# The latents' MLP of a two-layer hybrid trunk: eight block products per projection, or Strassen's seven

## The chip, the cores and the metric

The kernel runs on one NeuronCore of one Trainium2 chip. The metric is device time in microseconds (us) for one launch. Before the change it was 3617.11 us, the median of 3 runs (3616.78 to 3617.87).

## What is computed

The reference is a trunk of two layers over 1024 latent tokens and 256 context tokens with 1024 features. Each layer has a token mixer and then an MLP; what matters here is the MLP, its norms and its residual:

```python
def sq_relu_mlp(h, w1, w2):                      # w1: 1024 x 4096, w2: 4096 x 1024
    return jnp.square(jax.nn.relu(h @ w1)) @ w2

# per layer, after the token mixer gave y_lat (and y_ctx in layer 0)
h_lat = h_lat + gate_a * rms_norm(y_lat, norm_g[layer, 1])
m_lat = modulate(rms_norm(h_lat, norm_g[layer, 2]), shift_m, scale_m)
h_lat = h_lat + gate_m * rms_norm(sq_relu_mlp(m_lat, w_mlp1, w_mlp2), norm_g[layer, 3])
if need_ctx:  # layer 0 only: the same for the 256 context tokens, modulated by c_ctx
    ...
```

## The kernel before, in words

Data are feature-major: a tile holds 128 features on the partitions and tokens along the free axis. The tokens are cut into three chunks: 0 is the context (256 tokens), 1 and 2 are the latents (512 each). Every large product is done in three matmuls of fp32r operands: a number is split into a high part (a cast on ScalarE, ACT) and a low part (the difference, on VectorE, DVE), and high x high, high x low and low x high are added up in PSUM.

A weight tile is 128 x 512 (four blocks of 128 x 128). `split_w` (L176 to L184) loads it into one of three buffers `raw` (DMA issued on SyncE, SP), casts it to `wh` (L182, ACT) and takes the difference `wl` (L183, on DVE in the MLP). It has two buffers each of `wh` and `wl`. `proj` (L186 to L195) uses a weight tile for 12 matmuls per chunk.

A layer's second half goes: output projection (`po`), the norm between (`norm_mid`: post-norm with residual, then pre-norm), the MLP, the norm at its end (`norm_end`). The MLP goes over the tokens in passes: in layer 0 chunk 1, then chunks 2 and 0 together, so that one split weight tile serves 12 matmuls of 512 columns and 12 of 256; in layer 1 chunk 1, then chunk 2. In a pass `up` (tile `pu`) makes one block of 128 hidden features from two weight tiles, squares the ReLU and splits the result into `hh` and `hl`; `down` (tile `pd`) takes groups of four hidden blocks into the eight output blocks `y`, which are added up in SBUF (L1378). Hidden features never leave the chip.

The order on each engine is set by a scheduler from priorities and a timeline of its own; `aside` (L1278) gives the norms a lower priority than the matmuls that follow them. At the end of layer 1 the last `down` of chunk 2 is done in two halves of 256 tokens, each with its weights split anew, and then the last norm and the output's DMA follow.

Of the kernel before, what the change touches and what calls it, by code (L numbers as in the profile page):

```python
# [17 lines left out]
D = 1024  # L18
LT = 1024
LC = 256  # L20
# [77 lines left out]
def _prep(i):  # L98
# [23 lines left out]
    o["w2"] = f["w_mlp2"].reshape(DEPTH, 8, 4, 128, KB, 128).transpose(0, 1, 4, 3, 2, 5)  # L122
# [18 lines left out]
def kernel(ctx: ExitStack, tc: tile.TileContext, a: dict, out: bass.AP, dbg=None):  # L141
# [34 lines left out]
    def split_w(src, eng, b=128):  # L176
        n = src.shape[1]
        raw = wp.tile([128, 512], F32, tag="raw", name="raw")
        nc.sync.dma_start(out=raw[:, :n], in_=src)
        wh = wp.tile([128, 512], F32R, tag="wh", name="wh", bufs=2)  # L180
        wl = wp.tile([128, 512], F32R, tag="wl", name="wl", bufs=2)
        S.copy(out=wh[:, :n], in_=raw[:, :n])  # L182
        eng.tensor_tensor(out=wl[:, :n], in0=raw[:, :n], in1=wh[:, :n].bitcast(F32), op=SUB)  # L183
        return [w[:, :n].rearrange("p (a b) -> p a b", b=b) for w in (wh, wl)]  # L184

    def proj(src, pss, xs, eng):  # L186
        """pss[ci] = src^T x over the 8 blocks of 128 features, in three products of the operands' parts"""
        for g in range(2):
            wh, wl = split_w(src[:, 4 * g:4 * g + 4].rearrange("p a b -> p (a b)"), eng)
            for ci, ps in pss.items():  # L190
                n = CHUNKS[ci][1]
                for k in range(4):
                    for j, (w_, x_) in enumerate(((wh, xs[ci][0]), (wh, xs[ci][1]), (wl, xs[ci][0]))):
                        P.matmul(out=ps[:, :n], lhsT=w_[:, k], rhs=x_[:, 4 * g + k, :n],  # L194
# [13 lines left out]
    def ada(l, g, ap_, pp, sbp=None):  # L208
# [9 lines left out]
        sb = sbp.tile([128, 512], F32, tag="t2", name="asb", bufs=4) if sbp else ap_.tile([128, 512], F32, tag="asb", name="asb", bufs=1)  # L218
# [25 lines left out]
    def nrsqrt(ps, n, scale, tile_):  # L244
        """-1 / sqrt(scale * ps + EPS): the table's value and a Newton step"""
# [5 lines left out]
        V.scalar_tensor_tensor(out=y[:, :n], in0=h[:, :n], scalar=1.5, in1=y[:, :n], op0=SUB, op1=MULT)  # L251
        return y

    def rstd_of(src, n, tile_, pp):
        accs = []
        for half in range(2):
# [3 lines left out]
            for b in range(4 * half + 1, 4 * half + 4):  # L260
                sq = tile_("sq")
                S.activation(out=sq[:, :n], in_=src(b), func=AF.Square)  # L262
                eng.tensor_tensor(out=acc[:, :n], in0=acc[:, :n], in1=sq[:, :n], op=ADD)  # L263
            accs.append(acc)
# [3 lines left out]
        return nrsqrt(ps, n, 1.0 / D, tile_)  # L268

    def prenorm(l, w, y, c, hi, lo, tile_, pp):  # L270
        n = y.shape[2]
        s1, sh = mods[l][3][w], mods[l][0][:, 24 * w:24 * w + 8]
        r = rstd_of(lambda b: y[:, b], n, tile_, pp)
        for b in range(KB):
            q = tile_("q")
            V.scalar_tensor_tensor(out=q[:, :n], in0=y[:, b], scalar=s1[:, b, c:c + 1], in1=r[:, :n], op0=MULT, op1=MULT)
            if b % 4 == 3:
                S.activation(out=q[:, :n], in_=q[:, :n], func=AF.Identity, bias=sh[:, b, c:c + 1])
                S.copy(out=hi[:, b], in_=q[:, :n])
                G.tensor_tensor(out=lo[:, b], in0=q[:, :n], in1=hi[:, b].bitcast(F32), op=SUB)  # L280
                continue
            S.activation(out=hi[:, b], in_=q[:, :n], func=AF.Identity, bias=sh[:, b, c:c + 1])  # L282
            V.scalar_tensor_tensor(out=lo[:, b], in0=q[:, :n], scalar=sh[:, b, c:c + 1],  # L283
                                   in1=hi[:, b].bitcast(F32), op0=ADD, op1=SUB)

    def postnorm(l, w, y, c, hsrc, tile_, pp):
        """y = hsrc + gate * normalized y"""
        n = y.shape[2]
        res = not isinstance(hsrc, bass.AP) or hsrc.shape[0] == 128
        gg = mods[l][4][w]  # L290
        r = rstd_of(lambda b: y[:, b], n, tile_, pp)
        for b in range(KB):
            if res:
                ht = hsrc[:, b]
            else:
                ht = tile_("ht")
                nc.sync.dma_start(out=ht[:, :n], in_=hsrc[b])
            q = tile_("q")
            V.scalar_tensor_tensor(out=q[:, :n], in0=y[:, b], scalar=gg[:, b, c:c + 1], in1=r[:, :n], op0=MULT, op1=MULT)  # L299
            G.tensor_tensor(out=y[:, b], in0=q[:, :n], in1=ht[:, :n], op=ADD)  # L300
# [18 lines left out]
    def gates(l, ap_, pool, prm):  # L319
        """raw [128, NU, 36] = dt(2,6) | a(2,6) | b(2,6) per token -> dt, a=dt*A, g, beta."""  # L320
# [1116 lines left out]
```

## Time and profile before

| | |
|---|---|
| median of 3 runs | 3617.11 us |
| profiled execution, span from its first to its last instruction | 3611.6 us |
| between that span and the median | 5.5 us |
| TensorE (PE) matmuls busy | 3329.6 us (92%), 21790 matmuls |
| DVE / ACT / GpSimd (POOL) busy | 2162.3 / 1606.0 / 1042.2 us |
| DMA | 497.96 MB, mean 138 GB/s |

The output projection and MLP of layer 0 run from about 880 to 1940 us, those of layer 1 from about 2754 us to the end. In both, PE's slices are at 8 and 9 tenths, and DVE's and ACT's at 2 to 6. A matmul's "busy" in this profile lasts from its issue to its modelled end, so that successive matmuls overlap: how many run in a stretch says what one costs, not the mean length of one.

### The profile page before, as it was taken

What the parts mean: (1) busy time and instruction counts of PE and PEld (TensorE: products, weight loads), DVE (VectorE), ACT (ScalarE), POOL (GpSimd) and SP (SyncE); (2) the same over time, 40 slices, a digit from 0 to 9 for tenths busy, and PEclk for the clock granted to TensorE, in tenths of its full rate; (3) what the DMA queues carried; (4) which work ended last, traced back from release to release, by engine and by line L of the source; (5) the groups of instructions that cost most, each with busy time, mean ns of one, the idle gap of its engine ahead of it and who ended that gap; (6) DMA issues with size and microseconds to landing.
All of it is one profiled execution on the core that took longest, in us unless ns stands there. A gap on an engine that the chain in (4) does not pass through costs nothing. (4 is left out here: it accounts for less than half of the span.)

```text
span 3611.6 us, 57569 instructions
## 1 busy us (share of the span) xinstructions
PE 3329.6 (92%) x21790; PEld 2648.5 (73%) x21790; DVE 2162.3 (60%) x3645; ACT 1606.0 (44%) x3059; POOL 1042.2 (29%) x993
## 2 busy tenths in 40 slices
PE   4998898999989999999998888888999899999997
PEld 2766786766866888888886566776677678877886
DVE  6668961487585446544438557982575764454445
ACT  4665533566463334322225465532665553333333
POOL 3238324574251001100005337533672420010002
PEclk8999999899999999999998899998999999999998
DMA  5467447664245333322223555636754333334333
GB/s 200 140 192 203 138 116 225 224 206 152 94 137 181 98 98 102 107 65 62 65 63 112 173 168 161 172 112 197 238 183 150 129 110 96 97 115 142 97 96 102
DMA packets 359324, 497.96 MB, mean 138 GB/s; under 512 B 62998, under 2 KB 220550, under 8 KB 359046
## 3 DMA queue, kind: packets, MB, share of 16 engines
q1 hardware_dynamic: 356166, 480.12, 43.0%
q0 software_dynamic: 2880, 14.16, 1.3%
q8 instruction: 171, 2.80, 0.3%
q14 instruction: 107, 0.88, 0.1%
HBM read 387.09 MB, written 107.07 MB: 137 GB/s over the span
## 5 line engine op out<-in xcount | busy, mean ns | idle before, releaser
L182 ACT CAST wh<-raw 128x512 fp32r<-128x512 f32 (+1 forms) x712 | 440.1, 619 | 1019.6 <-PE pd L1372 475.6
L183 DVE TENSOR_TENSOR wl<-raw,wh 128x512 fp32r<-128x512 f32 x592 | 425.2, 720 | 407.1 <-ACT wh L182 389.7
L263 POOL TENSOR_TENSOR nacc<-nacc,nsq 128x256 f32<-128x256 f32 (+1 forms) x105 | 95.6, 912 | 1468.8 <-ACT nsq L262 1466.2
L1372 PE MATMUL pd<-hh,wh 128*128 128x512 f32 (+1 forms) x1312 | 481.6, 367 | 11.2 <-DVE y L1378 7.2
L1372 PE MATMUL pd<-hh,wl 128*128 128x512 f32 (+1 forms) x1312 | 480.5, 368 | 7.3 <-DVE wl L183 7.3
L194 PE MATMUL pu<-th,wl 128*128 128x512 f32 (+1 forms) x1280 | 475.0, 371 | 11.8 <-DVE wl L183 11.8
L194 PE MATMUL pu<-th,wh 128*128 128x512 f32 (+1 forms) x1280 | 477.4, 373 | 7.0 <-ACT th L282 7.0
L1372 PE MATMUL pd<-hl,wh 128*128 128x512 f32 (+1 forms) x1312 | 479.2, 365 | 0.2 <-DVE hl L1360 0.2
L194 PE MATMUL pu<-tl,wh 128*128 128x512 f32 (+1 forms) x1280 | 475.2, 371 | 3.2 <-DVE tl L283 3.2
L194 PE MATMUL ps<-th,wh 128*128 128x512 f32 (+1 forms) x1144 | 440.8, 387 | 19.7 <-ACT ub L371 7.8
L194 PE MATMUL ps<-th,wl 128*128 128x512 f32 (+1 forms) x1144 | 430.6, 379 | 6.5 <-POOL wl L183 6.5
L194 PE MATMUL ps<-tl,wh 128*128 128x512 f32 (+1 forms) x1144 | 433.1, 379 | 0.0
L1378 DVE TENSOR_TENSOR y<-pd,y 128x512 f32<-128x512 f32 (+1 forms) x288 | 179.3, 624 | 305.2 <-PE pd L1372 305.0
L386 DVE SCALAR_TENSOR_TENSOR sil<-ub,cw,sil 128x256 f32<-128x256 f32 (+1 forms) x236 | 273.0, 1179 | 51.7 <-ACT sil L384 45.7
L183 POOL TENSOR_TENSOR wl<-raw,wh 128x512 fp32r<-128x512 f32 (+1 forms) x120 | 181.0, 1510 | 404.1 <-ACT wh L182 384.4
L1372 PEld LDWEIGHTS pd<-hh,wh 128*128 128x128 f32 x1312 | 249.5, 190 | 56.4 <-ACT wh L182 9.4
L1372 PEld LDWEIGHTS pd<-hh,wl 128*128 128x128 f32 x1312 | 249.1, 190 | 54.5 <-DVE wl L183 13.5
L194 PEld LDWEIGHTS pu<-th,wl 128*128 128x128 f32 x1280 | 243.0, 190 | 57.3 <-DVE wl L183 16.2
L194 PEld LDWEIGHTS pu<-th,wh 128*128 128x128 f32 x1280 | 243.4, 190 | 51.8 <-ACT th L282 7.8
L194 PEld LDWEIGHTS ps<-th,wh 128*128 128x128 f32 x1144 | 225.8, 198 | 73.5 <-issue 13.0
L1372 PEld LDWEIGHTS pd<-hl,wh 128*128 128x128 f32 x1312 | 249.6, 190 | 38.9 <-DVE hl L1360 0.4
L194 PEld LDWEIGHTS pu<-tl,wh 128*128 128x128 f32 x1280 | 243.2, 190 | 44.7 <-DVE tl L283 4.0
(291 smaller groups left out, 5946.1 us busy)
## 6 DMA issues: line engine op xcount, KB each, us to landing
raw<-in_w_dram SPq DMA_DIRECT2D x528, 256.0 KB
aw<-in_wada_dram SPq DMA_DIRECT2D x96, 512.0 KB
raw<-in_winf_dram SPq DMA_DIRECT2D x116, 256.0 KB
stp<-rt SPq DMA_DIRECT2D x36, 768.0 KB
raw<-in_wout_dram SPq DMA_DIRECT2D x64, 256.0 KB
rt<-st SPq DMA_DIRECT2D x72, 192.0 KB
crow<-rc POOLq DMA_DIRECT2D x36, 384.0 KB, 4.8
sr<-rs SPq DMA_DIRECT2D x18, 576.0 KB
```

The lines of the kernel that those rows point to most:

```text
L182: S.copy(out=wh[:, :n], in_=raw[:, :n])
L183: eng.tensor_tensor(out=wl[:, :n], in0=raw[:, :n], in1=wh[:, :n].bitcast(F32), op=SUB)
L194: P.matmul(out=ps[:, :n], lhsT=w_[:, k], rhs=x_[:, 4 * g + k, :n], start=(g + k + j == 0), stop=(g == 1 and k == 3 and j == 2))
L263: eng.tensor_tensor(out=acc[:, :n], in0=acc[:, :n], in1=sq[:, :n], op=ADD)
L386: V.scalar_tensor_tensor(out=acc, in0=u[:, o + k:o + k + n], scalar=w[:, bi, k:k + 1], in1=acc, op0=MULT, op1=ADD)
L1372: P.matmul(out=ps[:, :n], lhsT=w_[:, k], rhs=x_[:, o:o + n], start=(i == 0), stop=(i == 11))
L1378: V.tensor_tensor(out=y, in0=ps[:, :n], in1=y, op=ADD)
```

## The change

The latents' MLP is done by Strassen's scheme (Winograd's form): weights and tokens are cut in halves along both axes of a product, so that 7 products of quarter size, on sums of quarters, stand for 8. Chunks 1 and 2 are the two token halves. Context tokens no longer share weight tiles with chunk 2 and get a pass of their own with the old scheme (`up0`, `down0`) after the latents'.

For the inner layer's 16 pairs of hidden blocks, `up(i)` makes four sums of weight tiles on DVE (S1, S2, `A11`-`A21`, `A12`-S2) and up to seven products, with token operands B11, B21, B22, T1 to T4 that stay in SBUF. From the four results, which it squares, it makes the seven operands that the outer layer needs, and stores them to DRAM (`th`, 256 KB each). Two of the seven products (`begin`) need chunk 1 alone; for the first 8 (layer 0) or 10 (layer 1) pairs they are done ahead (`ahead`), beside the norms of chunk 2, and what doesn't fit in PSUM goes through DRAM (`tp`). The outer layer goes through 4 groups of 7 steps: a step loads a hidden operand of 1 MB from DRAM and splits it (`hidden`), makes sums of weights in SBUF (`make`), and does four weight tiles' products for all 512 columns.

```diff
+    def two(raw, eng, b=128):
...
+        pool = wps[0]
+        wps.append(wps.pop(0))
+        wh = pool.tile([128, 512], F32R, tag="wh", name="wh", bufs=2)
+        wl = pool.tile([128, 512], F32R, tag="wl", name="wl", bufs=2)
+        S.copy(out=wh[:, :n], in_=raw)
+        eng.tensor_tensor(out=wl[:, :n], in0=raw, in1=wh[:, :n].bitcast(F32), op=SUB)
...
+            def product(ps, wts, ops, first=True):
+                wh, wl = wts
+                for j in range(4):
+                    xh, xl = ops[j]
+                    for i, (w_, x_) in enumerate(((wh, xh), (wh, xl), (wl, xh))):
+                        P.matmul(out=ps, lhsT=w_[:, j], rhs=x_, start=first and j + i == 0, stop=(j == 3 and i == 2), skip_group_check=True)
...
+            def begin(i, A11, A12):
+                b1, b2 = bank(), bank()
+                product(b1, two(A11, V), B11)
+                p1 = granule("p1")
+                S.copy(out=p1, in_=b1)
+                if HELD <= i < BEGUN:
+                    nc.sync.dma_start(out=tp[l][i], in_=p1)
+                h11 = granule("h11")
+                product(b2, two(A12, V), B21)
+                V.tensor_tensor(out=h11, in0=b2, in1=p1, op=ADD)
+                square(h11, h11)
+                put_h(i, 0, h11)
...
+            def up(i, beside=lambda: None):
...
+                product(b1, two(S2, V), T2, False)
...
+                S.copy(out=h12, in_=b1)
...
+                product(b3, two(S1, V), T1)
...
+                S.copy(out=h22, in_=b3)
...
+                V.tensor_tensor(out=A11, in0=A11, in1=A21, op=SUB)
+                product(b1, two(A11, V), T3, False)
...
+                V.tensor_tensor(out=h22, in0=b1, in1=h22, op=ADD)
+                square(h22, h22)
+                put_h(i, 2, h22)
+                V.tensor_tensor(out=A12, in0=A12, in1=S2, op=SUB)
+                product(b3, two(A12, V), B22, False)
...
+            STEPS = ((0, 0, (0, 0), 0, "S1"), (1, 1, (0, 0), 1, "S2"), ("S2", 4, (1, 0), 0, "S3"), (0, 5, (1, 1), 0, None),
+                     (3, 6, (0, 1), 0, "S4"), ("S1", 3, (1, 1), 2, None), (1, 2, (1, 0), 2, None))
...
+                for m in range(4):
+                    ps = banks[bk][m]
+                    wts = two(W[g, w_][:, m], V)
+                    product(ps, wts, [[t[:, j] for t in ops2[g, k][1:]] for j in range(4)], fresh)
+                    if g == 0 and bk == 0:
+                        S.copy(out=y[:, m], in_=ps)
+                    else:
+                        V.tensor_tensor(out=y[:, m], in0=ps, in1=y[:, m], op=ADD)
+                    if m == 0 and beside:
+                        make(beside, g)
+                    if m in (0, 1) and n_ + 1 < len(todo):
+                        hidden(todo[n_ + 1][0], todo[n_ + 1][2], 2 * m)
+                if last and g == 3 and k == 6:
+                    aside(lambda: run(end(1, 0, 512, lat(1), nte)))
...
+                def down0(g):
+                    for m in range(KB):
+                        wh, wl = split_w(a["w2"][l, g // 2, 2 * (m // 4) + g % 2][:, m % 4].rearrange("p a b -> p (a b)"), V)
+                        for j in range(4):
+                            hh, hl = hid[8 * (g // 2) + 2 * j + g % 2]
+                            for i, (w_, x_) in enumerate(((wh, hh), (wh, hl), (wl, hh))):
...
+                                P.matmul(out=acc[m], lhsT=w_[:, j], rhs=x_, start=(g + j + i == 0 and m % 2 == 0),
+                                         stop=(g == 7 and j == 3 and i == 2), skip_group_check=True)
+                        if m % 2:
+                            run(both, 1)
```

`two` splits a weight tile or a sum that is in SBUF, with buffers from two pools in turn, so that four pairs of `wh` and `wl` are in use. `up` begins with four loads and S1 and S2. `both` is a generator: the end norms of chunks 1 and 2 (512 columns at a time, not 256 as before), a piece of which is emitted after each `up0` and every second output block of `down0`. Of the end of layer 1 the last norm now covers 512 tokens, and no weights are split twice. `split_w` keeps its three `raw` buffers.

Three places show how the order changed. On PE, in layer 0's outer layer before, each split weight tile served 512 columns of chunk 2 and then 256 of the context (`pd`, `hh` and `hl` are the hidden parts):

```order
L1372 MATMUL pd<-hl,wh 128x512
L1372 MATMUL pd<-hh,wl 128x512
L1372 MATMUL pd<-hh,wh 128x256
L1372 MATMUL pd<-hl,wh 128x256
L1372 MATMUL pd<-hh,wl 128x256
L1372 MATMUL pd<-hh,wh 128x256
```

The context's own pass in the changed kernel (`pu` is any PSUM bank of the MLP, `x` the context's operand parts, `nps` the sum of a latent chunk's norm):

```order
L204 MATMUL pu<-x_15658,wh 128x256
L204 MATMUL pu<-x_15659,wh 128x256
L204 MATMUL pu<-x_15658,wl 128x256
L295 MATMUL nps<-nacc,cst 128x512
L204 MATMUL pu<-x_15658,wh 128x256
```

There a weight tile is followed by 12 matmuls of 256 columns and no others. On SP in layer 0's MLP before, the queue held weight loads almost alone (`hl` and `hm` are the residual stream in DRAM):

```order
L179 DMA raw<-in_w_dram 128x512
L1313 DMA hl_96<-y 128x8x256
L179 DMA raw<-in_w_dram 128x512 x3
L1293 DMA res<-hm_95 128x8x512
L179 DMA raw<-in_w_dram 128x512 x115
```

In the changed kernel's inner layer, in the same queue, for pairs 11 to 13 of layer 0 (`A` a weight load; `th` a store, of h11, h22, u1, u2, h12, h21, u4):

```order
L1421 DMA th_118<-u_12712 128x512
L1412 DMA A<-in_w_dram 128x512
L1421 DMA th_119<-h_12769 128x512
L1412 DMA A<-in_w_dram 128x512 x2
L1421 DMA th_121<-h_12829 128x512
L1412 DMA A<-in_w_dram 128x512
L1421 DMA th_122<-u_12872 128x512
L1421 DMA th_123<-u_12873 128x512
L1421 DMA th_124<-h_12810 128x512
L1421 DMA th_120<-h_12897 128x512
L1421 DMA th_125<-u_12874 128x512
L1412 DMA A<-in_w_dram 128x512
```

The four loads of a pair now stand between seven stores, each of which waits for a result. On DVE in the outer layer before (`wl` a weight tile's low part, `y` a sum from PSUM):

```order
L1378 TENSOR_TENSOR y<-pd,y 128x512
L1378 TENSOR_TENSOR y<-pd,y 128x256
L183 TENSOR_TENSOR wl<-raw,wh 128x512
L1378 TENSOR_TENSOR y<-pd,y 128x512
L1378 TENSOR_TENSOR y<-pd,y 128x256
```

One step of the outer layer in the changed kernel (`x` is the low part of the next hidden operand, `S_14646` a sum of weights, `xb` the outputs and the weights):

```order
L193 TENSOR_TENSOR wl<-xb,wh 128x512
L1581 TENSOR_TENSOR S_14646<-S_14563,xb 128x1024 x2
L1650 TENSOR_TENSOR xb<-pu,xb 128x512
L193 TENSOR_TENSOR wl<-xb,wh 128x512
L1650 TENSOR_TENSOR xb<-pu,xb 128x512
L193 TENSOR_TENSOR wl<-xb,wh 128x512
L1596 TENSOR_TENSOR x<-x 128x1024 x2
L1650 TENSOR_TENSOR xb<-pu,xb 128x512
L193 TENSOR_TENSOR wl<-xb,wh 128x512
L1650 TENSOR_TENSOR xb<-pu,xb 128x512
```

Besides a difference and a sum per weight tile there are now two to four operations of 1024 columns per step, for the sums of weights and the split of the next operand.

## Rows read from the trace of the kernel before

**Rows 1.** The page, by engine: busy us (share of the span) xinstructions
```profile
PE 3329.6 (92%) x21790; PEld 2648.5 (73%) x21790; DVE 2162.3 (60%) x3645; ACT 1606.0 (44%) x3059; POOL 1042.2 (29%) x993
```

**Rows 2.** Stretches of the MLP: us, busy (xinstructions) by engine, clock, DMA share, GB/s
```profile
1200.00:1300.00 100.00, 100.00 (x443) 82.81 (x442) 48.28 (x74) 33.08 (x55) 0.00 (x0) 1.00 0.32 98
1700.00:1800.00 100.00, 100.00 (x576) 88.23 (x575) 42.29 (x73) 23.88 (x44) 0.00 (x0) 1.00 0.20 63
```

**Rows 3.** PE's groups by form: shapes xcount | busy us, mean ns | idle before
```profile
L194 PE MATMUL pu<-th,wh 128*128 128x512 f32 x1024 | 404.9, 395 | 7.0 <-ACT th L282 7.0
...
L1372 PE MATMUL pd<-hh,wh 128*128 128x512 f32 x992 | 388.5, 392 | 3.0 <-ACT wh L182 2.8
...
L1372 PE MATMUL pd<-hh,wh 128*128 128x256 f32 x320 | 93.1, 291 | 8.1 <-DVE y L1378 7.2 <-ACT wh L182 0.8
...
L194 PE MATMUL pu<-th,wh 128*128 128x256 f32 x256 | 72.5, 283 | 0.0
```

**Rows 4.** DVE's groups by form, whole span
```profile
L183 DVE TENSOR_TENSOR wl<-raw,wh 128x512 fp32r<-128x512 f32 x592 | 425.2, 720 | 407.1 <-ACT wh L182 389.7 <-DMA raw<-in_wout_dram 5.1 <-PE nps L267 3.3
...
L1378 DVE TENSOR_TENSOR y<-pd,y 128x512 f32<-128x512 f32 x216 | 149.0, 691 | 265.2 <-PE pd L1372 265.2
...
L1378 DVE TENSOR_TENSOR y<-pd,y 128x256 f32<-128x256 f32 x72 | 30.3, 422 | 40.1 <-PE pd L1372 39.8
...
L684 DVE TENSOR_TENSOR XX<-XX,Bi 128x1024 f32<-128x1024 f32 x8 | 13.0, 1651 | 0.0
```

**Rows 5.** Chain near the end (last half pass of chunk 2): start us, us, what
```profile
3572.43 0.63 ACT wh L182
...
3573.09 0.70 DVE wl L183
3573.81 3.47 DMA raw<-in_w_dram
...
3577.38 0.63 ACT wh L182
```

**Rows 6.** ACT there: start us, us, line op, idle before and its releaser
```profile
3575.31 0.62 ACT L182 CAST wh<-raw 128x512 fp32r<-128x512 f32 x1 [0.49 <-PE pd L1372]
...
3584.19 0.62 ACT L182 CAST wh<-raw 128x512 fp32r<-128x512 f32 x1 [1.72 <-PE pd L1372]
```

**Rows 7.** The same place in stretches, columns as in rows 2
```profile
3564.00:3576.00 12.00, 11.58 (x93) 11.14 (x92) 9.96 (x21) 8.26 (x18) 2.51 (x3) 1.00 0.53 153
3576.00:3588.00 12.00, 8.27 (x61) 7.59 (x59) 11.22 (x22) 5.51 (x12) 6.15 (x7) 0.96 0.32 90
```

**Rows 8.** PE after a wait there: successive matmuls of 256 columns
```profile
3589.18 0.58 PE L1372 MATMUL pd<-hh,wl 128*128 128x256 f32 x1 [0.81 <-DVE wl L183]
3589.55 0.41 PE L1372 MATMUL pd<-hh,wh 128*128 128x256 f32 x1
...
3591.05 0.41 PE L1372 MATMUL pd<-hl,wh 128*128 128x256 f32 x1
```

**Rows 9.** Transitions in stretches: layer 0; layer 1's start; layer 1 twice; columns as in rows 2
```profile
1000.00:1100.00 100.00, 84.82 (x347) 65.78 (x346) 84.16 (x144) 61.67 (x143) 47.70 (x48) 0.95 0.41 134
1940.00:2000.00 60.00, 42.72 (x155) 26.97 (x153) 53.15 (x78) 31.98 (x76) 41.15 (x48) 0.86 0.33 108
...
2780.00:2900.00 120.00, 103.55 (x417) 82.32 (x416) 82.27 (x142) 64.98 (x144) 47.24 (x47) 0.93 0.38 125
3200.00:3300.00 100.00, 95.64 (x412) 76.40 (x411) 57.18 (x88) 42.01 (x80) 19.51 (x22) 1.00 0.47 153
```

**Rows 10.** The chain's last pieces: start us, us, what
```profile
3593.85 0.44 DVE y L1378
...
3598.71 0.50 DVE nq L299
...
3599.28 6.07 POOL y L300 x7
```

**Rows 11.** The kernel's first 20 us in a stretch, columns as in rows 2
```profile
0.00:20.00 20.00, 1.22 (x2) 0.50 (x2) 4.53 (x19) 8.71 (x18) 2.69 (x8) 1.00 0.95 332
```

More of the change, by code (lines that the diff above doesn't have):

```diff
@@ L179, in split_w @@
         nc.sync.dma_start(out=raw[:, :n], in_=src)
[L180 to L183, printed above, removed]
+        return two(raw[:, :n], eng, b)
+    wps = [wp]
+    def two(raw, eng, b=128):
+        n = raw.shape[1]
+        pool = wps[0]
[4 more added lines that the diff above has]
+        eng.tensor_tensor(out=wl[:, :n], in0=raw, in1=wh[:, :n].bitcast(F32), op=SUB)
         return [w[:, :n].rearrange("p (a b) -> p a b", b=b) for w in (wh, wl)]
@@ new lines, in run, with outproj @@
+            def run(gen, n=1 << 20):
+                for _ in range(n):
+                    if next(gen, gen) is gen:
+                        return
+            def outproj(ci, beside=None, at=0):
+                y = new_y(ci)
+                for m in range(KB):
+                    if beside and m == at:
+                        beside()
+                    ps = bank()
+                    proj(a["wout"][l, m], {ci: ps}, mx, V)
+                    S.copy(out=y[m], in_=ps[:, :CHUNKS[ci][1]])
+                return y
@@ new lines @@
+            mx = {1: load_mix(1)}
+            y1 = outproj(1)
+            mx[2] = load_mix(2)
+            if not last:
+                mx[0] = load_mix(0)
+            B11, B21 = quarter(), quarter()
+            y2 = outproj(2, lambda: run(mid(1, y1, dict(enumerate(B11 + B21)))), 2)
+            if not last:
+                y0 = outproj(0)
+            B22, T1, T2 = quarter(), quarter(), quarter()
+            m2 = mid(2, y2, {4 + j: B22[j] for j in range(4)}, (4, 5, 6, 7, 0, 1, 2, 3))
+            begun = {}
@@ new lines, in ahead, with put @@
+            def ahead(n):
+                for _ in range(n):
+                    i = len(begun)
+                    if i < BEGUN:
+                        b1 = begin(i, *rows1(i, 0, 1))[0]
+                        begun[i] = b1 if i < HELD else None
+            dsh = mp.tile([128, 4], F32, tag=f"dsh{l}", name="dsh")
+            V.tensor_tensor(out=dsh, in0=sh1[:, 4:8, 0], in1=sh1[:, 0:4, 0], op=SUB)
+            def put(x, raw):
+                S.copy(out=x[0], in_=raw)
+                V.tensor_tensor(out=x[1], in0=raw, in1=x[0].bitcast(F32), op=SUB)
@@ new lines @@
+            run(m2)
+            for j in range(4):
+                put(T1[j], t1s[j])
+            ahead(1)
+            T3 = [(x[:, j], z[:, j]) for x, z in [(big(F32R), big(F32R))] for j in range(4)]
+            for j in range(4):
+                t3 = nt("t3")
+                V.scalar_tensor_tensor(out=t3, in0=y2[4 + j], scalar=dsh[:, j:j + 1], in1=y2[j], op0=ADD, op1=SUB)
+                put(T3[j], t3)
+            ahead(1)
+            for j in range(4):
+                t4 = y1[4 + j]
+                V.scalar_tensor_tensor(out=t4, in0=t4, scalar=sh1[:, 4 + j, 0:1], in1=t2s[j], op0=ADD, op1=SUB)
@@ new lines, with open_left @@
+            T4 = [(x[:, j], z[:, j]) for x, z in [(big(F32R), big(F32R))] for j in range(4)]
+            for j in range(4):
+                put(T4[j], y1[4 + j])
+            ahead(BEGUN)
+            def open_left(name, bufs):
+                el.close()
+                return el.enter_context(tc.tile_pool(name=f"{name}{l}", bufs=bufs))
+            early = iter(())
+            if last:
+                wa = open_left("wa", 1)
+            for i in range(16):
+                up(i, lambda: run(early, 1))
+                if i == 3 and not last:
+                    run(mid(0, y0, {}))
+                    nc.sync.dma_start(out=hy.rearrange("k p t -> p k t"), in_=y0t[0])
+                    ap_ = open_left("adae", 2)
+                    early = ada_steps(1, 0, ap_, el.enter_context(tc.tile_pool(name="adaep", bufs=1, space=PSUM)), granule)
+                if i == 14 and not last:
+                    run(early)
+                    wa = open_left("wa", 1)
@@ L1394, in end @@
[L1394 to L1414 removed]
+                        up0(blks[g + 1][0])
@@ L1415 @@
+                    down0(g)
+                    if g < 7:
+                        for b in blks[g + 1][1:]:
+                            up0(b)
+                run(both)
+                yc = new_y(0)
+                for m in range(KB):
+                    S.copy(out=yc[m], in_=acc[m])
+                tc.cur_priority += LOW + 10000
+                ahl[0] = hilo(0)
+                run(end(0, 0, 256, yc, nt))
+                ew.close()
+                wps[:] = [wp]
     hls.close()
```

470 lines of the change are left out of this document (300 added, 170 removed).

## The prediction

> **What bounds the kernel now.** I read the page's engine line first: PE's matmuls are busy 92% of the span, DVE 60%, ACT 44% [rows 1]. Busy matmuls overlap, so I went next to stretches, and counted. In the latents' pass PE runs 443 matmuls of 512 columns in 100 us without a gap, at clock 1.00, with DVE at 48 us, ACT at 33 us and DMA at 0.32 of its share; beside the context it runs 576, half of 512 and half of 256 columns [rows 2]. So a matmul of 512 columns costs 100/443 = 0.2257 us and a pair 100/288 = 0.3472, which leaves 0.1215 us for 256 columns. The MLP's steady state is TensorE and nothing else: whoever takes matmuls out of it takes their whole cost out, as long as the other engines keep up. Then I looked at where PE does wait: at the transitions [rows 9], and at the end, where single weight tiles serve only 256 columns [rows 5 to 7]. That last place matters most, because the change makes a whole pass of that kind.
>
> **The change part by part.** The durations are from the profiled execution, whose span is 3611.6 us; the median of the runs shown stands 5.5 us above it, and I add that at the end.
>
> *Matmuls.* Of 512 columns the MLP has 3 x 1024 in the inner and 3 x 992 in the outer layer, of 256 columns 3 x 256 and 3 x 320 [rows 3], or 6048 and 1728. After: per layer and projection 7 products x 16 x 12 = 1344, so 4 x 1344 = 5376 of 512 columns; the context keeps 768 + 768 = 1536 of 256 columns, and the 192 of layer 1's last halves become part of the products. That removes 672 x 0.2257 = 151.7 us and 192 x 0.1215 = 23.3 us: **-175.0 us**. Nothing is late behind them but the engines below, so each has a term.
>
> *The context's own pass* (layer 0, 128 weight tiles, 12 x 0.1215 = 1.46 us of PE each, 186.6 us in all, which was paid before too). A `raw` buffer is free when `wl` is done; near the end a load issued then took 3.47 us to land, then came the cast and the difference, and the same buffer's turn was 3577.38 - 3572.43 = 4.95 us [rows 5]. Three buffers give one tile per 1.65 us. With a norm beside, five tiles took 3584.19 - 3575.31 = 8.88 us, 1.78 each [rows 6]. The pass has norms beside it for most of its length, so I take 1.76: 128 x (1.76 - 1.46) = **+38 us**. Ends: +24 (1.65), and +142 if a tile went at the half-clock pitch, 12 x 0.2143 = 2.57 us [rows 8].
>
> The Trainium skill (DMA: Bandwidth & Descriptors, section Anatomy of one DMA) gives a fit, for DMAs issued from GpSimd, of a fixed 2.0 us plus the bytes at 436 GB/s. That would be an estimate of 2.6 us for 256 KB, a turn of 4.08 and a tile per 1.36 us, hidden under PE's 1.46; by it the term would be nothing. Here the loads are issued on SP, and the row's 3.47 us decides.
>
> *Outer layer's DVE.* A step has 48 matmuls, 10.83 us. On DVE it has four low parts at 0.72, four sums at 0.69, two differences of 1024 columns and, in four of seven steps, two sums of 1024. From 0.42 us at 256 columns and 0.69 at 512 a line gives 1.23 at 1024; an operation of that shape took 1.65 beside GpSimd [rows 4]. A step with `make` is 4 x 0.72 + 4 x 0.69 + 4 x 1.23 = 10.6 us, one without 8.1; at 1.65 they are 12.2 and 8.9. A group of seven is 66.7 of PE's 75.8 us, or 75.5 at worst, so DVE fits, narrowly. DVE takes its work in order, and a sum that waits for PSUM holds a low part behind it, which PE has up to four tiles of slack for. I take **+10 us** for both layers; ends 0 and 8 groups x 4 steps x (12.2 - 10.83) = +44.
>
> *Inner layer.* A pair's 84 matmuls are 19.0 us; DVE has at most 18 operations, 18 x 0.72 = 13.0; hidden. Its DMA is 4 loads and 7 stores, 2.9 MB in 19.0 us = 152 GB/s, and for pairs begun ahead about 3.1 MB in 60 x 0.2257 = 13.5 us = 230 GB/s, against 332 that the queue moved at a share of 0.95 [rows 11]. In layer 0 the modulation weights (16 of 512 KB) come on top of some of these pairs: 5.2 MB in 13.5 us would be more than 332 GB/s allows, 15.8 us, but in about four pairs alone. On SP the loads stand behind stores that wait for results, though about a pair ahead of their use. **+10 us** for all of this; ends 0 and the second rival's price.
>
> *Between output projection and MLP.* Before, 100 us of layer 0 held 347 matmuls and 120 us of layer 1 held 417: at 0.2257 at least 21.7 and 25.9 us are lost [rows 9]. After, chunk 2's norms and T1 to T4 need about 68 operations of DVE, the products begun ahead 3 each. Layer 1: (68 + 30) x 0.72 = 70.6 us against a cover of 10 x 24 x 0.2257 = 54.2; 16.4 are uncovered. Layer 0, with the context's projection (16 low parts) on both sides: (68 + 24 + 16) x 0.72 = 77.8 against 43.3 + 23.3 = 66.6; 11.2. Two norm sums in a row, 4.9 us each from the last y to the first scaling [rows 10], give DVE little to do: some 10 us per layer on top. 47.6 against 47.6: **0**, ends -20 and +30.
>
> *Pass boundary of layer 1.* 412 in place of 443 matmuls [rows 9] is 7 us that goes with the second pass: **-7**. In layer 0 the context's pass takes its place. The inner layer's first weights for the outer one are loaded well before by SP's order, so I cost that seam at nothing; uncovered, it is one load, some 5 us a layer.
>
> *Start of layer 1.* 155 matmuls in 60 us, 25 us lost at least [rows 9], waiting for norms that ended with the context's. After, both latent chunks are normed during the context's pass, and their 2 x 72 matmuls (32.5 us) stand ahead of the context's: **-12**, ends -25 and +5.
>
> *Tail.* From the last sum to the first scaling 4.9 us, then 6.7 us on GpSimd for 256 columns [rows 10]. With 512: 4.9 x 0.69/0.42 = 8.0, and 12 DVE operations x 0.72 = 8.6: **+5**, ends 0 and +12.
>
> Sum: -175 + 38 + 10 + 10 + 0 - 7 - 12 + 5 = -131. 3611.6 - 131 + 5.5 = **3486 us**.
>
> **The rivals.**
>
> 1. *Half clock in the context's pass.* After a wait of 0.81 us matmuls of 256 columns went at 0.2143 us, the lower of the two levels, 1.2 GHz [rows 8]. If the pass's waits keep the clock there, the term is +142 in place of +38: 3590. Against it: in the stretch where PE waited a little for each tile the clock was 1.00, and 0.96 where waits were longer [rows 7]. The Trainium skill (TensorE: Matmul & The Clock Gate, The HAM clock gate) says that the throttled clock is the default and activity lifts it, which is this rival's mechanism; the trace agrees that both levels occur. 5%.
>
> 2. *SP's queue holds the weights back: slower.* In each of 32 pairs the loads stand behind stores that wait for products. If each pair lost one turn of a load, 4.95 us [rows 5], that is 158 in place of 10: 3611.6 - 131 + 148 + 5.5 = 3634. It makes the kernel slower by more than 0.2% from (131 + 10 + 7)/32 = 4.6 us a pair. For it: seven waiting stores per pair in the order. Against: five `A` buffers let loads run about a pair ahead. 4%.
>
> 3. *DVE binds.* Outer layer at the upper price (+44), transitions at theirs (+30): 3486 + 34 + 30 = 3550. DVE near its limit speaks for it; GpSimd's idleness there (0.00 busy in the steady rows [rows 2]) against. 10%.
>
> 4. *Loads and DVE are hidden after all.* If a load of the context's pass lands within 2.9 us, a turn is 4.38 and three buffers give a tile per 1.46 us, PE's own pace; if the inner and outer layer run like the steady rows too [rows 2], the three terms go to nothing: 3486 - 58 = 3428. 3.47 us [rows 5] speaks against. The rule on DMAs cited above would have the landing so. 8%.
>
> That the scheme saves fewer products than it says is no rival: the order holds 5376 matmuls of the new kind.
>
> **How the numbers follow.** The forecast has 73%, the rivals 27%. Its own range is 3450 to 3540. For 8 in 10 I go from 3440, short of rival 4, to 3560, which takes in rival 3. What a measurement of this kernel can tell from no change is about 0.2%, 7 us. Faster: the forecast and rivals 1, 3 and 4, 96%, less 1 for the upper end of rivals 1 and 3 together; within 0.2%: 1%; slower: rival 2, 4%.
>
> **What would show it.** Matmuls of 512 columns in the MLP fall to 5376 and still come at 443 per 100 us in the inner and outer layer of either latents' part; at under 430 in the outer layer, with DVE over 95 of 100 us, rival 3 holds. The context's pass shows some 225 us for 1536 matmuls, with casts waiting for loads; at clock 0.5 it is rival 1, at 187 us rival 4. In the inner layer, waits of PE that end in an `A` load are rival 2. At the start of layer 1 the first 60 us should hold some 30 more matmuls. I am wrong if the latents' 5376 matmuls take over 1280 us (they need 1213).

## The result, and the profile after

The changed kernel takes 3518.4 us (median of four runs, 3516.2 to 3522.3) against 3616.95 us (3614.7 to 3617.9): a ratio of 0.9728, 95% interval 0.9714 to 0.9742. That is faster, inside the forecast's range, and 32 us above the forecast's 3486 us. A second set of runs, z2_after below, gave 0.9718 (0.9701 to 0.9736).

The page of the profiled execution (span 3520.5 us), by engine, shows TensorE still as the busiest engine, with 892 instructions fewer on it, and VectorE's share up from 60 to 67% [rows 1]:

```profile
PE 3174.7 (90%) x20898; PEld 2512.8 (71%) x20898; DVE 2359.9 (67%) x3729; ACT 1792.9 (51%) x3195; POOL 932.9 (26%) x825
```

Stretches of the changed kernel, columns as in [rows 2]; the outer layer's steady part in layer 0 and in layer 1:

```profile
1500.00:1600.00 100.00, 100.00 (x443) 82.81 (x442) 78.45 (x102) 40.13 (x55) 0.00 (x0) 1.00 0.47 160
3280.00:3380.00 100.00, 100.00 (x443) 82.81 (x442) 75.35 (x100) 41.48 (x57) 0.00 (x0) 1.00 0.48 162
```

443 matmuls in 100 us without a gap, as before, beside a VectorE that went from 48 to 75 and 78 us. TensorE's groups by form answer [rows 3]:

```profile
L1405 PE MATMUL pu<-x,wh 128*128 128x512 f32 x3072 | 955.9, 393 | 32.4 <-ACT wh L192 15.6 <-DVE x L1516 4.8 <-ACT p L1428 4.1
L1405 PE MATMUL pu<-x,wl 128*128 128x512 f32 x1536 | 595.4, 392 | 1.8 <-DVE wl L193 1.8
...
L1405 PE MATMUL pu<-xb,wh 128*128 128x512 f32 x512 | 165.8, 405 | 12.9 <-ACT h L1455 10.7 <-DVE h L1469 1.0 <-issue 0.8
...
L1405 PE MATMUL pu<-xb,wl 128*128 128x512 f32 x256 | 102.3, 400 | 0.0
```

3072 + 1536 + 512 + 256 are the 5376 matmuls of the seven products; TensorE's idle time before all of them is 47 us. VectorE's two new kinds, where [rows 4] had only an estimate of mine and a neighbour:

```profile
L1596 DVE TENSOR_TENSOR x<-x 128x1024 fp32r<-128x1024 f32 x112 | 132.0, 1219 | 25.8 <-PE pu L1405 19.8 <-ACT x L1595 5.9
L1650 DVE TENSOR_TENSOR xb<-pu,xb 128x512 f32<-128x512 f32 x192 | 131.3, 684 | 51.3 <-PE pu L1405 51.1
```

To see where the time went, both profiled executions are divided at the same four matmuls: the first of layer 0's output projection, the first of layer 1's input projection, the first of layer 1's output projection, the last of the MLP. TensorE before and, below, after (start us, us, what, idle before it and its releaser):

```profile
880.49 0.47 PE L194 MATMUL po<-th,wh 128*128 128x512 f32 x1
...
1940.27 0.39 PE L428 MATMUL ps<-th,wl 128*36 128x512 f32 x1
...
2753.57 0.49 PE L194 MATMUL po<-th,wh 128*128 128x512 f32 x1 [3.31 <-ACT th L1274]
...
3593.39 0.41 PE L1372 MATMUL pd<-hh,wl 128*128 128x256 f32 x1
```

```profile
909.82 1.62 PE L204 MATMUL pu<-x,wh 128*128 128x512 f32 x3 [6.70 <-ACT x L1341]
...
1931.82 0.65 PE L453 MATMUL ps<-x,wh 128*36 128x512 f32 x2 [0.74 <-ACT y L1725]
...
2739.23 1.65 PE L204 MATMUL pu<-x,wh 128*128 128x512 f32 x3 [6.74 <-ACT x L1341]
...
3480.00 0.40 PE L1405 MATMUL pu<-x,wl 128*128 128x512 f32 x1
```

| stage | before, us | after, us | difference | the forecast's terms for it |
|---|---|---|---|---|
| A: start to layer 0's output projection | 880.5 | 909.8 | +29.3 | 0 |
| B: to layer 1's input projection | 1059.8 | 1022.0 | -37.8 | -86.7 + 38 + 5 + 5 = -39 |
| C: to layer 1's output projection | 813.3 | 807.4 | -5.9 | -12 |
| D: to the last matmul of the MLP | 839.8 | 740.8 | -99.0 | -65.0 - 23.3 + 5 + 5 - 7 = -85 |
| E: to the end | 18.2 | 40.5 | +22.3 | +5 |
| sum | 3611.6 | 3520.5 | -91.1 | -131 |

(Of 512 columns 384 matmuls leave layer 0, 86.7 us, and 288 leave layer 1, 65.0 us, where 192 of 256 columns, 23.3 us, go too.) B came out as forecast and D 14 us better; what is missing lies in A, E and, with 6 us, in C, and of these A had no term at all. The spans differ by 91.1 us where the medians differ by 98.6: the profiled execution before lay 5.5 us under its median, this one 2.1 us over it. So 40 us are missing from the spans and 32 from the medians.

D's 14 us were mostly lost by the kernel before, at its end. The 192 matmuls of its two last half passes, priced at 23.3 us, ran from 3560.0 to 3593.4 us:

```profile
L1372 PE MATMUL pd<-hh,wh x64: 278/283/551, 3560.0 to 3593.0; 128*128 128x256 f32 x64
```

They took 33.4 us, and [rows 7] has a part of it: 61 matmuls in the 12 us from 3576 us.

In the tail, two norms of 512 columns stand one behind the other. Everything but transfers after the last matmul, cut to its turning points:

```profile
3480.24 1.02 PE L295 MATMUL nps<-nacc,cst 128*128 128x512 f32 x2
3481.36 0.69 ACT L262 ACTIVATE ny<-nps,epst 128x512 f32<-128x512 f32 x1 [11.41 <-PE nps L295]
...
3495.59 4.13 POOL L290 TENSOR_TENSOR nacc<-nacc,nsq 128x512 f32<-128x512 f32 x3 [1.81 <-ACT nsq L289]
...
3500.50 2.08 PE L295 MATMUL nps<-nacc,cst 128*128 128x512 f32 x2 [19.24 <-DVE nacc L294]
...
3513.44 1.64 POOL L324 TENSOR_TENSOR xb<-nq,xb 128x512 f32<-128x512 f32 x1 [0.27 <-DVE nq L323]
```

The first `nps` is chunk 1's, although its outputs were complete some 21.7 us earlier: the norm had been put at a lower priority than the matmuls (`aside` around `end(1)`), so its sum over the partitions got its place in TensorE's order behind all of them. (21.7 us are two steps of 48 matmuls at 0.2257.) Chunk 2's `nps` comes 20.3 us later. [Rows 10] had the last norm, of 256 columns, there alone.

In stage A, SP's queue in the changed kernel issues the loads of the mixer's output only at 903 us:

```profile
903.15 0.37 SPq L1338 DMA_DIRECT2D xb<-rm  x1
903.61 1.23 SPq L1143 DMA_DIRECT2D rm<-amix  x2
904.89 0.59 SPq L1338 DMA_DIRECT2D xb<-rm  x1
```

Before, the same queue had its loads out 50 us earlier, and their casts were done while attention still ran. That kernel's first projection matmul, at 880.49 us, stood ahead of the attention's last 18 matmuls, which take about 3 us (here the last six of them); after, it stands behind all of them, so that these 3 us moved from stage B to stage A:

```profile
853.16 0.88 SPq L1272 DMA_DIRECT2D y<-rm  x2
...
891.55 1.08 PE L1113 MATMUL aop<-aPT,attv 128*64 128x256 f32 x6
```

The new pools are bigger in one piece: ten operand buffers on one side and seven on the other. My theory was that the last buffer on either side reaches into the memory of the attention's pools, so that the whole pool waits for that memory's last reader, the attention's last matmul; x2_loads tests it.

### The profile page after: what moved, and what is told of

Its sections match the earlier page's. It is cut to its first block, busy times and chain, and to the rows that moved or that the text cites. A ratio compares the mean times of both kernels' runs of the same rounds, so it can differ in the third digit from the quotient of the medians.

```text
span 3520.5 us, 56161 instructions
## 1 busy us (share of the span) xinstructions
PE 3174.7 (90%) x20898; PEld 2512.8 (71%) x20898; DVE 2359.9 (67%) x3729; ACT 1792.9 (51%) x3195; POOL 932.9 (26%) x825
## 5 line engine op out<-in xcount | busy, mean ns | idle before, releaser
L1405 PE MATMUL pu<-x,wh 128*128 128x512 f32 x3072 | 955.9, 393 | 32.4 <-ACT wh L192 15.6
L204 PE MATMUL ps<-x,wh 128*128 128x512 f32 (+1 forms) x2288 | 687.9, 384 | 15.7 <-ACT ub L396 8.2
L1405 PEld LDWEIGHTS pu<-x,wh 128*128 128x128 f32 x3072 | 578.8, 189 | 167.2 <-ACT wh L192 22.5
L1405 PE MATMUL pu<-x,wl 128*128 128x512 f32 x1536 | 595.4, 392 | 1.8 <-DVE wl L193 1.8
L204 PEld LDWEIGHTS ps<-x,wh 128*128 128x128 f32 x2288 | 425.6, 198 | 107.3 <-issue 21.0
L204 PE MATMUL ps<-x,wl 128*128 128x512 f32 (+1 forms) x1144 | 431.9, 380 | 7.9 <-POOL wl L193 7.9
L192 ACT CAST wh<-raw 128x512 fp32r<-128x512 f32 (+1 forms) x328 | 200.8, 616 | 312.5 <-PE ps L204 88.1
L1405 PEld LDWEIGHTS pu<-x,wl 128*128 128x128 f32 x1536 | 290.3, 189 | 65.5 <-DVE wl L193 3.4
L204 PE MATMUL pu<-x,wh 128*128 128x256 f32 (+1 forms) x1152 | 285.9, 341 | 21.4 <-ACT x L1341 13.4
L193 DVE TENSOR_TENSOR wl<-raw,wh 128x512 fp32r<-128x512 f32 x208 | 149.9, 728 | 144.0 <-ACT wh L192 137.2
L204 PEld LDWEIGHTS pu<-x,wh 128*128 128x128 f32 x1152 | 201.9, 196 | 48.6 <-issue 10.0
L192 ACT CAST wh<-A 128x512 fp32r<-128x512 f32 x192 | 118.7, 619 | 148.6 <-PE pu L1405 141.6
```

Of the source, the lines that this page charges most:

```text
L192: S.copy(out=wh[:, :n], in_=raw)
L193: eng.tensor_tensor(out=wl[:, :n], in0=raw, in1=wh[:, :n].bitcast(F32), op=SUB)
L204: P.matmul(out=ps[:, :n], lhsT=w_[:, k], rhs=x_[4 * g + k][:, :n], start=(g + k + j == 0), stop=(g == 1 and k == 3 and j == 2))
L1405: P.matmul(out=ps, lhsT=w_[:, j], rhs=x_, start=first and j + i == 0, stop=(j == 3 and i == 2), skip_group_check=True)
```

## The experiments

Every run was timed beside the kernel before, in five rounds; 0.001 of the ratio is 3.6 us. The changed kernel stands at 0.9728 and 0.9718.

**x1_tail.** The end norm of chunk 1 at the matmuls' own priority:

```
-   aside(lambda: run(end(1, 0, 512, lat(1), nte)))
+   run(end(1, 0, 512, lat(1), nte))
```

> Only the place of chunk 1's end norm in layer 1 is changed: it stands beside the last two steps of the outer layer instead of behind them. Theory (the tail holds two norms of 512 columns one after the other): the stretch from the last MLP matmul to the end falls from 40.5 us to about 24 us, the time from 3518 to about 3502 us (3496 to 3508). Rival (the last two steps are full on VectorE, so that the norm's operations hold the products up by as much as they save behind): 3513 to 3519 us, with the last matmul of the MLP 10 us or more later.

3500.5 us, 0.9681 (0.9667 to 0.9695). The MLP's last matmul starts at 3465.0 of 3495.2 us: 30.2 us are left in place of 40.5, not the 24 I expected, and the outer layer of layer 1 took 310.4 us from its first product to its last, in place of 310.2. TensorE there:

```profile
3475.23 2.08 PE L295 MATMUL nps<-nacc,cst 128*128 128x512 f32 x2 [9.84 <-DVE nacc L294]
```

One wait of 9.84 in place of 19.24 us: one norm went under the matmuls, at no cost to them. The tail's theory holds.

**x2_loads.** Operand pool 9 + 1, buffer pool 6 + 1, so that the large parts end short of the attention's memory, and one weight pool for the first output projection:

```
-   HL[0] = ...tile_pool(name=f"hl{i}", bufs=10)
+   HL[0] = ...tile_pool(name=f"hl{i}", bufs=9);  HL[1] = ...tile_pool(name=f"hm{i}", bufs=1)
-   xb = ...tile_pool(name=f"xb{l}", bufs=7, side="right")
+   xb = ...(bufs=6, side="right");  xl = ...(name=f"xl{l}", bufs=1, side="right")
-   wps[:] = [wp, mw]          (ahead of the first output projection)
+   wps[:] = [wp, mw]          (behind it)
```

> The operands' pool is 9 + 1 buffers in place of 10 and the buffer pool on the other side 6 + 1 in place of 7, so that neither of the big parts lies on the attention's memory; the first output projection's weights use one pool alone. Theory (the loads of the mixer's output and their casts waited for the attention's last matmul because of the memory): the first output projection matmul of layer 0 stands some 10 us earlier against the attention's end and half of that again in layer 1; 3508 us (3502 to 3513). Rival (they wait for the attention's data): 3515 to 3521 us, the loads issued at the same place behind the attention's last matmul.

3527.6 us, 0.9755 (0.9742 to 0.9768): 10 to 13 us slower than the changed kernel. The loads did move, to 864 us:

```profile
864.00 0.91 SPq L1339 DMA_DIRECT2D xb<-rm  x2
```

But the first projection matmul stands 17.1 us behind the attention's last score matmul where it stood 18.9: it comes behind all of attention in TensorE's order anyway. The wait before it fell from 6.70 to 0.51 us, but the attention's own end took longer: the casts, now early, stood among its copies on ScalarE (2.18 us for four of them), TensorE waited for such a copy, and its last matmuls had a mean granted clock of 0.64, where the changed kernel had 1.00 for its own (x2_loads, then the changed kernel):

```profile
895.53 1.12 PE L1138 MATMUL aop<-aPT,attv 128*64 128x256 f32 x2 [2.27 <-ACT aPT L1133]
...
896.00:903.00 7.00, 6.49 (x25) 3.02 (x23) 2.52 (x5) 3.48 (x7) 0.00 (x0) 0.64 0.00 0
```

```profile
895.00:903.00 8.00, 7.02 (x36) 3.25 (x34) 0.00 (x0) 5.09 (x10) 0.00 (x0) 1.00 0.16 40
```

Then the projection waited 5.3 us for weights, which now came late, and in layer 1 the wait grew from 6.7 to 14.9 us:

```profile
2747.38 1.52 PE L204 MATMUL pu<-x,wh 128*128 128x512 f32 x2 [14.88 <-ACT x L1342]
```

So the pools' place in memory was what held the loads back, as the theory said, and with it gone the first projection matmul came under 2 us earlier against the scores: what stood behind that wait took the rest. The run changes the weights' pool too; z3_loads2 leaves that part out.

**x3_pools.** Layer 0's input projection gets its operands in one pool per chunk, as before. The mixer of layer 0 then has the order of the kernel before on TensorE, up to the last scores:

```
+   for ci in (1, 2, 0):
+       H0[ci] = ...tile_pool(name=f"hl{ci}_0", bufs=2)
-   ahl[ci] = hilo(ci)
+   ahl[ci] = hilo0(ci)
```

> The operands of layer 0's input projection lie in one pool for each chunk, as in the kernel before; this gives the mixer of layer 0 the order of the kernel before back, all else is the changed kernel's. Theory (the changed order of the mixer costs the 19 us by which the attention's last scores of layer 0 stand later than before, less the 6 us that are there already at the input projection's end): 3505 us (3499 to 3510), the last scores at 872 to 878 us. Rival (the lag is not from the order): 3515 to 3521 us with the last scores at 888 us or later.

3507.3 us, 0.9699 (0.9676 to 0.9722), with runs from 3491 to 3519; the interval touches the changed kernel's. Attention's score matmuls of layer 0 (count, ns, first and last start), here, and below in x1_tail, which has the changed kernel's order:

```profile
L1101 PE MATMUL asc<-attk,aq x72: 362/406/668, 671.5 to 878.0; 128*128 128x256 f32 x48, 128*128 128x384 f32 x24
```

```profile
L1101 PE MATMUL asc<-attk,aq x72: 362/384/690, 669.5 to 877.7; 128*128 128x256 f32 x48, 128*128 128x384 f32 x24
```

The times hardly differ. In the changed kernel's first profile the last of them was at 890.9, before at 872.1. Over the nine profiles with the changed kernel's order on TensorE up to there it lies between 877.7 and 890.9, mean 883.8; over the three with the old order (this, z1_best, z3_loads2) at 875.7 to 878.0, mean 876.9. So about 7 of the first profile's 19 us belong to the order, on a spread of 13 us for one and the same order.

**x4_norms.** In the context's pass the end norms advance half as often:

```
+   if len(hid) % 2:
        run(both, 1)
-   if m % 2:
+   if m % 4 == 3:
        run(both, 1)
```

> The end norms beside the context's pass advance half as often, so that they are spread over the whole pass. Theory (norms on VectorE hold up the pass's first half, 2.3 us a tile against 1.54 us in the second): the pass falls from 219 us to about 200 us, the time to about 3503 us (3498 to 3510). Rival (three raw buffers and their loads bind the whole pass): the pass stays at 214 to 222 us and the time at 3515 to 3521 us.

3513.6 us, 0.9716 (0.9700 to 0.9732). From its first to its last matmul the pass took 233.6 us where the changed kernel took 234.9 (the 219 and 221 us in the expectations leave out the pass's first or last tiles). But the edit did not spread the norms. Their sums on TensorE, in the changed kernel and here, stand 12 to 96 us into the pass in both:

```profile
L295 PE MATMUL nps<-nacc,cst x8: 590/592/697, 1707.9 to 1792.2; 128*128 128x512 f32 x8
```

```profile
L295 PE MATMUL nps<-nacc,cst x8: 590/592/697, 1698.6 to 1782.8; 128*128 128x512 f32 x8
```

So the run says nothing about the theory, for or against; why the pieces kept their place is not shown. What the casts of the weights wait for in the pass stayed too, 59.1 us here against, in the changed kernel (engine, group, releaser: us, times, longest):

```profile
ACT wh L192 <- DMA raw<-in_w_dram: 55.5, 55, 3.7
```

**y1_raw6.** Six raw buffers there in place of three:

```
-   raw = wp.tile([128, 512], F32, tag="raw")
+   raw = raws[0].tile([128, 512], F32, tag="raw", bufs=3);  raws.append(raws.pop(0))
-   nt = lambda nm: cm.tile(..., bufs=8)
+   nt = lambda nm: cm.tile(..., bufs=5);  raws.append(cm)
```

> The context's pass loads its weights into six raw buffers in place of three (the norms' scratch there falls from eight to five). Theory (the turn of three raw buffers binds the pass: its casts wait 55 us for loads, and spreading the norms did not shorten it): the pass falls from 221 us to 190 to 205 us and the time to about 3497 us (3488 to 3506). Rival (the norms' work on VectorE beside, or the rate of the loads themselves, binds): the pass stays at 214 to 222 us, the time at 3512 to 3520 us.

3502.1 us, 0.9686 (0.9669 to 0.9703). The pass took 209.8 us, and the casts' waits for loads are gone; they wait for TensorE:

```profile
ACT wh L193 <- PE pu L1702: 34.4, 38, 2.7
```

The same 40 us of the span, 24 and 29 us into the pass, first in the changed kernel and then here (columns as in [rows 2]):

```profile
1720.00:1760.00 40.00, 30.11 (x173) 27.76 (x174) 33.40 (x51) 27.08 (x54) 16.24 (x9) 0.79 0.54 181
```

```profile
1720.00:1760.00 40.00, 37.00 (x288) 35.10 (x289) 38.40 (x54) 32.22 (x65) 10.87 (x7) 1.00 0.56 189
```

With norms beside, 288 matmuls in place of 173, VectorE at 38 of 40 us and the clock at 1.00. The pass in two halves of 64 tiles, which the norms divide (they end some 120 us into the changed kernel's pass); the changed kernel, then this run:

```profile
1695.90:1832.60 136.70, 112.10 (x777) 104.54 (x776) 107.54 (x157) 86.90 (x174) 39.50 (x24) 0.91 0.49 160
1832.60:1931.00 98.40, 95.83 (x770) 93.11 (x768) 49.84 (x81) 57.84 (x122) 1.70 (x3) 1.00 0.56 180
```

```profile
1691.00:1806.00 115.00, 102.99 (x778) 97.34 (x777) 104.84 (x145) 81.59 (x166) 37.73 (x22) 0.97 0.60 202
1806.00:1901.00 95.00, 93.05 (x770) 92.31 (x768) 59.36 (x95) 62.57 (x130) 6.17 (x5) 1.00 0.52 177
```

Beside the norms three buffers gave a tile per 2.14 us and six per 1.80; in the other half, nearly free of them, 1.54 and 1.48. The turn of three buffers bound the half with norms; of what is left there, VectorE is at 105 of 115 us. The pass gave 25 us, the time 12 to 15: stage C took 822.5 us in this profile. The twelve profiles of this document's versions have 801.5 to 823.6 us there, so that one profile doesn't tell whether this is spread.

**y2_three.** x1_tail, x4_norms and y1_raw6 together.

> Three edits together: chunk 1's end norm beside the last two steps, six raw buffers in the context's pass, and the norms there spread over the whole pass. Theory (they add up): 14 us from the tail and some 25 us from the pass, 3478 us (3470 to 3490). Rival (the pass does not get shorter): 3498 to 3506 us, what the tail's edit gave alone.

3489.9 us, 0.9656 (0.9639 to 0.9672); pass 209.0 us. Against 0.9723, the mean of the changed kernel's two ratios, that is 24 us, where the three alone make 15, 3 and 13: within their intervals the gains add up, at the upper end of what I expected.

**y4_cut.** One of the outer layer's seven products keeps a quarter of its matmuls:

```
-   for j in range(4):                                  (in product)
+   for j in range(nj):
-   product(ps, wts, [...], fresh)
+   product(ps, wts, [...], fresh, 1 if k == 3 else 4)
```

> It leaves out three quarters of the matmuls of one of the seven products of the outer layer, 36 of 48 in each of four groups and both layers, 288 matmuls or 65.0 us at 0.2257 us; every load, cast, sum and addition to the outputs stays. Theory (the matmuls set the outer layer's time and VectorE has room): 53 to 65 us less than the changed kernel, 3453 to 3466 us. Rival (VectorE, at 73 to 80 per cent there, is nearly the bound: the shortened step has 8 us of its work in 2.7 us): 30 to 45 us less, 3473 to 3488 us.

3464.5 us, 0.9590 (0.9566 to 0.9613). That is 46 to 50 us less by the ratios, between the theory and the rival. From its first product to its last the outer layer took 287.0 and 285.8 us in the two layers, in place of 311.1 and 310.2: 48.5 of the 65 us. (In the other profiles without added stores it lies between 309.6 and 313.6.) VectorE is then at 87:

```profile
1500.00:1600.00 100.00, 97.99 (x423) 78.42 (x422) 87.23 (x114) 43.90 (x61) 0.00 (x0) 1.00 0.50 175
```

Matmuls set most of the time there, but a quarter of what was taken out did not come out of it. TensorE's waits in the two outer layers, 14 us, end mostly on the cast of a weight tile; whether VectorE or ScalarE binds next is not shown.

**y5_stores.** Every store of the inner layer's sums twice:

```
    nc.sync.dma_start(out=th[l][i // 4][k][i % 4], in_=h)
+   nc.sync.dma_start(out=tw[l][k, i], in_=h)
```

> Each store of the inner layer's sums to DRAM is issued twice, the second time to memory that nothing reads: 224 stores of 256 KB more. Theory (the inner layer's transfers are hidden beside its matmuls, with the queue and the engines at 50 to 76 per cent): 0 to 6 us more than the changed kernel, 3515 to 3525 us. Rival (the transfers or the issuing queue are near the bound there, so that part of the inner layer's price is the way through DRAM): 15 to 40 us more, 3533 to 3560 us.

3536.3 us, 0.9786 (0.9769 to 0.9804): the rival, with 21 to 25 us by the ratios, about 0.1 us for each of 224 stores. In the profiles layer 0's products took 11.3 us more and layer 1's 20.6. Where layer 0's inner layer starts, in the changed kernel and here:

```profile
1140.00:1240.00 100.00, 94.92 (x487) 69.40 (x486) 59.69 (x96) 52.28 (x93) 0.00 (x0) 0.98 0.85 300
```

```profile
1140.00:1240.00 100.00, 89.25 (x445) 67.01 (x446) 48.80 (x75) 45.43 (x77) 0.00 (x0) 0.95 0.96 349
```

The transfer engines went from 0.85 to 0.96, matmuls from 487 to 445. The inner layer's sums go through DRAM with little room left. The added stores stand in SP's queue too, between the loads; the run doesn't tell that queue from the engines.

**z2_after.** The changed kernel again.

> The changed kernel itself, a second time and on the chip of z1_best, to see how far its stages move from run to run. Theory (the attention of layer 0 ended 13 us later in its first profile than in that of x1_tail, whose program is the same up to there, so this is spread): the first output projection matmul of layer 0 at 896 to 903 us of the span and the time at 3512 to 3520 us. Rival (the late mixer belongs to this program): 907 us or later.

3512.7 us (3509.6 to 3523.9), 0.9718. Its profiled execution was the slowest of the five, and its first output projection matmul stands at 906.3 us, between theory and rival. The lateness of stage A is thus part spread, part the program's.

**z1_best.** y2_three with x3_pools.

> The three edits of y2_three and the chunk-wise pools of x3_pools together. Theory (the gains add up): 26 us and some 4 to 10 us under the changed kernel, 3481 us (3473 to 3490). Rival (the pools gave nothing, what they showed was the spread of the runs): 3487 to 3494 us, as y2_three.

3477.1 us, 0.9623 (0.9606 to 0.9640), against y2_three's 0.9656: some 12 us, which with x3_pools speaks for the mixer's order, though in neither do the intervals part.

**z3_loads2.** z1_best with x2_loads' pools, but both weight pools from the start.

> z1_best with the 9 + 1 and 6 + 1 buffers of x2_loads, but with both weight pools from the output projection's start as in the changed kernel. Theory (x2_loads lost on what was moved with the loads, 6 us of weights in layer 0, and on the scan's last store in layer 1): the first output projection matmul of layer 0 stands 14 to 17 us behind the last scores in place of 18.5, the output projection takes 122 us again, and the time is 3467 to 3477 us. Rival (the loads' place decides nothing, since the attention's own tail and the queue behind it end there anyway): 3474 to 3484 us.

3470.0 us (3455.4 to 3476.5), 0.9595 (0.9573 to 0.9617). The first projection matmul stands 15.8 us behind the last scores, the output projection took 120.6 us. This is the fastest version that does all the work; whether the loads' place did it is open, since its interval overlaps z1_best's.

## Why the prediction was right

The four largest misses are +29 in A, +17 in E, +10 in the context's pass and -14 in D. That the sum came within 32 us owes something to the last of them, which was luck.

*The matmuls, -175.* Right: 5376 of the new kind, at 443 per 100 us in the outer layers. y4_cut shows from the other side that further matmuls taken out of the outer layer come out of the time to three quarters only.

*The context's own pass, +38.* The wait was right, its size short: 234.9 us are 1.84 us a tile and +48, where I had chosen 1.76. Neither of the two prices behind that choice held: three buffers alone gave 1.54 us a tile and not 1.65, beside norms 2.14 and not 1.78, and the norms stood beside half of the pass and not most of it. With six buffers the pass is 25 us shorter, 22 of them in the half with norms. By the Trainium skill (DMA: Bandwidth & Descriptors, Anatomy of one DMA) three buffers would, as an estimate, have been enough for 1.36 us a tile, and the pass would have been TensorE's own 186.6 us. The trace does not agree beside the norms, 2.14 us, and comes near without them, 1.54. The clock in the pass fell to 0.79 in one stretch and was 0.96 to 1.00 in others, so rival 1 did not come.

*Outer layer's VectorE, +10.* From the first sum into the outputs to the last matmul the two layers took 299 and 300 us for 1291 and 1299 matmuls, 291.4 and 293.2 at 0.2257: 14.4 us lost. The 1024-column operation took 1.219 us on my estimate of 1.23. Rival 3 did not come; with a seventh of the matmuls nearly gone, in y4_cut, VectorE was at 87 of 100 us.

*Inner layer, +10.* Its steady stretches lost 7.9 and 2.8 us. The 7.9 are no wait: 64 matmuls of layer 1's modulation stand in that stretch, 7.8 us at 0.1215, and TensorE had no gap from 1200 to 1300 us. y5_stores shows that this term lives on the room of the transfers or of their queue; the 332 GB/s that I took for the limit is none, for a stretch there moved 349.

*Between output projection and MLP, 0.* The difference was right, both of its sides were not. After:

```profile
1032.00:1200.00 168.00, 141.30 (x562) 0.95 0.67 229
...
2830.00:3000.00 170.00, 149.34 (x607) 0.95 0.57 197
```

(the products' own matmuls; us, busy, clock, DMA share, GB/s). 562 and 607 at 0.2257 are 126.8 and 137.0 us, so 41 and 33 us are lost where I had 47.6 in all. That put the 5376 products at 1314 us, over the 1280 that I had named as proof against me. But [rows 9] had shown me only a part of the old transitions. Counted alike, from the first matmul of the output projection to 1200 us in layer 0 and to 3000 us in layer 1, 53.5 and 37.9 us were lost before, 53.3 and 37.1 after. In all of stage B 69.8 of 1059.8 us were lost before (3456 matmuls at 0.2257 and 1728 at 0.1215 are 990.0) and 118.7 of 1022.0 after: 48.9 more, where the terms said 48. The terms were 17 us short, most of it in the context's pass, but the kernel before had lost 16 us from 1200 us to the stage's end, 10 of them in the last 40 us, for which I had no term. In D 58.1 us were lost before and 47.4 after, where the terms said 3 more; the end of the last half passes, 10 us, is most of that.

*Start of layer 1, -12.* Not decided. The first 60 us hold 236 matmuls, 81 more than in [rows 9]:

```profile
1931.80:1991.80 60.00, 46.34 (x236) 29.03 (x237) 22.65 (x40) 21.83 (x44) 21.77 (x28) 0.86 0.44 146
```

At the input projection's last matmul, 585.7 us into C where before had 588.3, most of that lead was gone, and C gained 5.9 us only, less than its spread between profiles. At its end stands the 6.74 us wait for the mixer's output, where before had 3.31.

*Tail, +5.* Mis-sized: +22.3. I priced one norm at 512 columns in place of 256, and did not look where the other chunk's norm stands in TensorE's order. x1_tail takes 10 us of it back by taking that low priority away; the 12 that are left are the upper end of what I gave the one norm.

*What had no term: stage A.* The first profile had +29.3 us there, the other eight profiles with this order +16 to +26. In the first profile 18.8 us are the later last scores, and about 7 of them belong to the mixer's changed order; the rest is within the spread of executions. The other 10.5 stand between the last scores and the first projection matmul, 18.9 us against 8.4: 6.70 are the wait for the casts of loads that memory held back, and about 3 the attention's matmuls that stood in stage B before. Neither the order nor the wait is in a line that the diff marks as the mixer's: pools that are laid out anew decide when loads may start and in which order the work before them is put.

Rival 2 did not come: no wait of TensorE in the inner layer ends in a weight load (VectorE's waits for one are 10.9 us in layer 0). What y5_stores shows is how near it was.

## What to carry to other kernels

A matmul saved on a TensorE-bound stretch is worth its full pitch as long as no other engine is close behind (three quarters of it in y4_cut); the surprises come from the stages the change doesn't name. Look at where every pool lies and whose memory it takes over, and at where low-priority work ends up in the order of the engine that it must pass through. A wait that is removed is worth what stands behind it: the early loads gave 2 us of an expected 10. Look in the trace, too, whether an edit moved what it was to move before its time is read as an answer: in x4_norms it had not. And count what was lost before over the whole stage, not in one stretch of it.

## What the runs showed that I had not expected

The mixer's matmuls, in one and the same order, ended 13 us apart in different profiles (877.7 to 890.9 us), so one profile's stage can't carry a difference of that size. 224 additional stores of 256 KB that nothing waits for cost about 0.1 us each; in the stretch shown the transfer engines' share had been 0.85 without them.
